# A hybrid layer on one core: the softmax of the next head issued ahead of the transposes and product of this one

## The chip, the core and the metric

The kernel runs on one core of a Trainium2 chip. TensorE (PE) multiplies matrices and writes to PSUM; VectorE (DVE), ScalarE (ACT) and GpSimd (POOL) do the rest, SyncE (SP) issues the loads of weights. Each engine takes its instructions strictly in the order that the program fixed for it. The metric is the time of one execution in microseconds (us), lower is better.

## The reference: what is computed

A decoder layer with two branches over 16 meta tokens and 512 real tokens, all in 32-bit floats. After a norm, one projection `u @ w_in` feeds a Mamba-2 branch (four groups) and an attention branch of 16 heads of 64. The attention is

```
s = q . k / 8 + (cq[t] - ck[s]),  masked to s <= t
p = softmax(s);  o = p @ v;  y_att = o * silu(z_att)
merged = g_ssd * (y_ssd @ w_proj_ssd) + g_att * (y_att @ w_proj_att)
out = x + rmsnorm(merged @ w_out)
```

The softmax goes in blocks of 128 queries: four blocks of real queries, block i with 16 + 128(i+1) keys, of which the first 16 are the meta tokens.

## The kernel before, in words

Every number is split into a high and a low part, and a product is made of three products of parts. The function `gemm` (its matmuls are on line L106) does this for all projections: 24 matmuls of 512 columns for the real tokens (`real_tokens`), 48 of 264 columns for all tokens (`all_tokens`). Its weights come as tiles `raw` (load on SP, L89), are split by ACT into `whi` (L90) and by DVE into `wlo` (L91, 1.2 us each), two buffers each. Its results lie in the PSUM tiles `mm`, of which there are two; a third product starts when the first one has been read.

All else on PE uses the PSUM tiles `ax`, one bank each, of which there are four.

The program runs the four groups of the Mamba-2 branch (`ssd_core`, with the sum of squares on L501 and its spread on L509 at a group's end), then the attention stage, eight pairs of heads (`att_pair`), with products of `s_group` and `gates` in between, then `gates` of the attention, `a_part`, and the output product (L747). The time of each instruction on its engine is fixed by a scheduler before the run, which takes the code's order as priority; parts in `raised()` go first. So while a head's softmax is under way on DVE and ACT, PE is given L106 matmuls of later projections, in an order that is then fixed.

One pair: products for q, k, v and the gate z (`zt`); q and k are evacuated by ACT (L539, L549, L550) and DVE (L540, L551); v is transposed (L558 for the meta tokens, L560). Then, head by head (`att_head`), five score pieces on four `ax` banks (L602 and L603); DVE masks each and takes its maximum (L605); ACT exponentiates (L608); DVE divides by the sum (L615). PE transposes the probabilities: ten blocks of 128x128 (L625), and four times the first 32 columns (L622), which hold the 16 meta columns, into a bank of their own, `t0`. ACT and DVE split the four transposed tiles into high and low parts (L635, L636), POOL zeroes the rest of the meta tile (L633), and nine matmuls (L648) make the product `po`. L582 to L590 gate the result and split it.

Of the kernel before, what the change touches and what calls it, by code (L numbers as in the profile page):

```python
# [37 lines left out]
def hybrid_kernel(ctx, tc, x, meta, norm_pre, w_in, conv_w, conv_b, dt_bias, a_log, d_skip,  # L38
# [490 lines left out]
    def att_pair(pr):  # L529
        heads2 = (2 * pr, 2 * pr + 1)  # L530
        q1, q2, k1, k2 = {}, {}, {}, {}
        ps = real_tokens(wcols(C_Q + pr * P))
# [43 lines left out]
        if pr % 4 == 0:  # L576
            ya[pr // 4] = (st("yhi", [P, 4, T], BUFS["y"], F32R), st("ylo", [P, 4, T], BUFS["y"], F32R))
        yt, lt = row("tmp", (P, T)), row("tmp", (P, T))
        for e in range(2):
            po = att_head(heads2[e], e, q1, q2, k1, k2, vv)  # L580
            m, l = slice(64 * e, 64 * e + 64), slice(64 - 64 * e, 128 - 64 * e)
            S.copy(lt[m], po[l])  # L582
            V.tensor_add(yt[m], po[m], lt[m])
        V.scalar_tensor_tensor(yt, yt, 0.5, zt, op0=ALU.mult, op1=ALU.mult)
        kk = pr % 4
        yh, yl = ya[pr // 4]
        if dbg is not None:
            nc.sync.dma_start(out=dbg["y_att"][pr], in_=yt)
        S.copy(yh[:, kk], yt)
        V.tensor_sub(yl[:, kk], yt, yh[:, kk].bitcast(F32))  # L590

    def att_head(hd, e, q1, q2, k1, k2, vv):
# [49 lines left out]
        for p in (ph, pl):
            seq += [(vv[:, 1, vs], p[1], 0),
                    (vv[:, 2, vs], p[2][:, 0:384], P), (vv[:, 3, vs], p[3], 2 * P),
                    (vv[:, 4, vs], p[2][:, 384:512], 3 * P)]
# [166 lines left out]
```

## Time and profile before

| | us |
|---|---|
| median of 3 runs (lowest, highest) | 861.39 (859.81, 862.04) |
| the profiled execution | 861.74 |
| its span, first to last instruction | 860.0 |
| PE busy in the span | 840.7 |
| DVE busy | 594.4 |
| ACT busy | 433.3 |
| POOL busy | 69.4 |

The profile is of one execution. Matmuls overlap in it: a matmul's row shows the time from its start to its modelled end, and the next one starts before that. What a matmul takes of PE's time is therefore read from the starts of neighbouring rows, not from its own length.

### The profile page before, as it was taken

The page shows a single profiled execution, that of the slowest core. Times are in us where ns is not written, and L with a number is a line of the kernel's source. Part 1 is how long each engine was busy: PE and PEld are TensorE (multiplying, and loading weights), DVE is VectorE, ACT ScalarE, POOL GpSimd, SP SyncE. Part 2 cuts the span into 40 slices and gives each one's busy share as a digit, 9 for nine tenths or more (in the row PEclk, how much of TensorE's full clock was granted, in tenths as well). Part 3 has the DMA queues.
Part 4 walks back from the last instruction along what each step waited for, and adds up shares of the span by engine and source line. Part 5 has one row for each costly group of instructions (what it writes and reads, how often), then busy time and mean ns, then how long its engine had stood idle before and what let it go on. Part 6 is the DMA issues. An engine that isn't in the chain of part 4 may idle for free.

```text
span 860.0 us, 13236 instructions
## 1 busy us (share of the span) xinstructions
PE 840.7 (98%) x5085; PEld 728.2 (85%) x5085; DVE 594.4 (69%) x1216; ACT 433.3 (50%) x834; POOL 69.4 (8%) x136
## 2 busy tenths in 40 slices
PE   6999999999999999999999999999999999999996
PEld 4998888778987799777889898989899988888885
DVE  6799598946985689656766565666667564568735
ACT  6455455446632465334435565656567564543332
POOL 3030110010000100011001000000001000000000
PEclk9999999999999999999999999999999999999999
DMA  7245353335323443212222313232323222224422
GB/s 212 75 130 156 88 105 104 97 81 117 99 84 88 108 113 94 78 50 77 74 74 75 100 51 99 52 98 52 97 55 96 75 74 75 73 74 147 148 74 98
DMA packets 114499, 79.94 MB, mean 93 GB/s; under 512 B 5684, under 2 KB 108260, under 8 KB 114436
## 3 DMA queue, kind: packets, MB, share of 16 engines
q1 hardware_dynamic: 110692, 70.08, 28.4%
q0 software_dynamic: 3744, 9.01, 5.0%
q8 instruction: 40, 0.66, 0.3%
q14 instruction: 23, 0.19, 0.1%
HBM read 76.65 MB, written 2.44 MB: 92 GB/s over the span
## 4 chain that ended last, share of the span: by engine, by line
PE 89%; DVE 4%; DMA 3%; issue 2%; ACT 0%; POOL 0%; SPq 0%; DVEq 0%; POOLq 0%
PE mm L106 70%; PE ax L648 3%; PE mm L747 3%; PE ax L625 2%; DMA big<-acs_d 2%; PE ax L747 1%; PE ax L482 1%; PE ax L467 1%; PE ax L603 1%; PE ax L602 1%; PE ax L457 1%; PE ax L441 1%; PE ax L622 1%; DMA big<-in_x_dram 1%; DVE big L452 1%
## 5 line engine op out<-in xcount | busy, mean ns | idle before, releaser
L106 PE MATMUL mm<-ulo,whi 128*128 128x264 f32 (+1 forms) x1024 | 286.5, 328 | 0.0
L106 PE MATMUL mm<-uhi,whi 128*128 128x264 f32 (+1 forms) x1024 | 283.8, 327 | 0.5 <-DVE xbc L551 0.5
L90 ACT CAST whi<-raw 128x1024 fp32r<-128x1024 f32 x118 | 124.2, 1053 | 151.7 <-PE mm L106 96.5
L106 PE MATMUL mm<-uhi,wlo 128*128 128x264 f32 (+1 forms) x1024 | 189.0, 326 | 0.0
L106 PEld LDWEIGHTS mm<-uhi,whi 128*128 128x128 f32 x1024 | 173.0, 189 | 18.0 <-issue 2.9
L106 PEld LDWEIGHTS mm<-ulo,whi 128*128 128x128 f32 x1024 | 173.1, 189 | 16.5 <-issue 2.7
L91 DVE TENSOR_TENSOR wlo<-raw,whi 128x1024 fp32r<-128x1024 f32 x117 | 142.7, 1220 | 61.0 <-ACT whi L90 32.7
L106 PEld LDWEIGHTS mm<-uhi,wlo 128*128 128x128 f32 x1024 | 153.4, 188 | 15.5 <-issue 0.7
L106 PE MATMUL mm<-yhi,whi 128*128 128x512 f32 x192 | 78.6, 410 | 0.7 <-ACT ms L666 0.7
L106 PE MATMUL mm<-ylo,whi 128*128 128x512 f32 x192 | 76.6, 399 | 0.0
L608 ACT ACTIVATE tmp<-tmp,nmx 128x264 f32<-128x264 f32 (+3 forms) x80 | 41.3, 517 | 32.1 <-DVE nmx L605 27.1
L385 DVE SCALAR_TENSOR_TENSOR xbc<-xp,hcol,xbc 128x528 f32<-128x528 f32 x72 | 54.0, 762 | 0.5 <-ACT tmp L388 0.3
L106 PE MATMUL mm<-yhi,wlo 128*128 128x512 f32 x192 | 53.8, 400 | 0.0
L636 DVE TENSOR_TENSOR big<-ax,big 32x512 fp32r<-32x512 f32 (+1 forms) x64 | 37.3, 616 | 23.2 <-ACT big L635 22.6
L452 DVE TENSOR_SCALAR big<-big,dtok 128x128 f32<-128x128 f32 x128 | 28.4, 286 | 26.7 <-DMA big<-acs_d 26.7
L605 DVE CUSTOM_DVE_ANT_0 tmp<-ax,maskf 128x264 f32<-128x264 f32 (+3 forms) x80 | 32.5, 431 | 20.8 <-PE ax L603 20.4
L461 ACT ACTIVATE tmp<-ax,eac 128x64 f32<-128x64 f32 x128 | 28.2, 330 | 35.2 <-PE ax L457 35.2
L106 PEld LDWEIGHTS mm<-yhi,whi 128*128 128x128 f32 x192 | 36.1, 188 | 10.7 <-issue 2.3
L106 PEld LDWEIGHTS mm<-ylo,whi 128*128 128x128 f32 x192 | 36.1, 188 | 9.4 <-issue 2.6
L106 PEld LDWEIGHTS mm<-yhi,wlo 128*128 128x128 f32 x192 | 35.8, 188 | 9.4 <-issue 2.2
L635 ACT CAST big<-ax 32x512 fp32r<-32x512 f32 (+1 forms) x64 | 28.9, 521 | 26.7 <-PE ax L622 26.6
L668 DVE TENSOR_TENSOR ms<-ms,mm 128x512 f32<-128x512 f32 x24 | 16.5, 686 | 25.4 <-PE mm L106 25.4
(255 smaller groups left out, 1134.0 us busy)
## 6 DMA issues: line engine op xcount, KB each, us to landing
raw<-in_w_in_dram SPq DMA_DIRECT2D x88, 512.0 KB, 3.6
big<-acs_d POOLq DMA_DIRECT2D x16, 512.0 KB, 6.0
raw<-in_w_proj_ssd_dram SPq DMA_DIRECT2D x16, 512.0 KB, 3.3
raw<-in_w_proj_att_dram SPq DMA_DIRECT2D x8, 512.0 KB, 3.4
raw<-in_w_out_dram SPq DMA_DIRECT2D x8, 512.0 KB, 3.4
big<-in_x_dram SPq DMA_DIRECT2D x4, 512.0 KB, 7.1
yhi<-in_x_dram SPq DMA_DIRECT2D x2, 1024.0 KB, 7.3
out_dram<-big SPq DMA_DIRECT2D x3, 512.0 KB, 2.6
```

Of the source, the lines that this page charges most:

```text
L90: S.copy(hi, raw)
L91: (GP if nparts[0] <= 1 else V).tensor_sub(lo, raw, hi.bitcast(F32))
L106: PE.matmul(o, lw, u[:, a:b], start=i == 0, stop=i == len(seq) - 1)
L385: V.scalar_tensor_tensor(o, xp[:, k:k + L], cw[:, 24 * k + ct:24 * k + ct + 1], o, op0=ALU.mult, op1=ALU.add)
L452: V.tensor_scalar(ab[:, i], ab[:, i], ac_t[:, c, g * HG + i:g * HG + i + 1], 0.0, op0=ALU.subtract, op1=ALU.min)
L461: S.activation(y[:, i * 64:(i + 1) * 64], py[:, i * 64:(i + 1) * 64], AF.Copy, scale=eac[:, c, g * HG + i:g * HG + i + 1])
L605: V.tensor_tensor_reduce(pr[i][:, a:b], o, m, -1.0, 3e38, ALU.add, ALU.min, nmx[:, n:n + 1])
L608: S.activation(pr[i][:, a:b], pr[i][:, a:b], AF.Exp, bias=nmx[:, i:i + 1], scale=-1.0, accum_out=rsum[:, n:n + 1])
L635: S.copy(h, src)
L636: V.tensor_sub(l, src, h.bitcast(F32))
L648: PE.matmul(po[:, o:T], w, p, start=i == 0, stop=i == len(seq) - 1)
L747: PE.matmul(pss[s][t], a, b, start=kq == 0 and i == 0, stop=kq == 3 and i == len(seq) - 1)
```

## The change

`att_pair` is taken apart into `att_qk`, `att_v`, `att_z`, `att_soft` (scores and softmax of one head) and `att_head` (transposes, product and evacuation of one head). The main loop writes `att_soft` of a head ahead of `att_head` of the one before it. The first v projection comes ahead of the first q and k; `s_group(3)` comes after the second pair instead of the first, and the `gates` of the SSD branch one pair later.

The five score pieces lie on three `ax` banks instead of four; the last block is cut into 240 and 288 columns instead of 264 and 264.

The meta columns are divided by the sum and split before they are transposed: for each of the four blocks ACT writes 16 high columns and DVE 16 low ones into one tile `mcol` of 128 columns, which one transpose brings into the spare part of bank `t3`. Four copies of 32 partitions (two on ACT, two on DVE) put the four blocks into the zeroed tile `meta`. So that this fits, the meta tokens of v are repeated eight times (`trep`, a copy on POOL) and transposed as 128 columns, which replaces a zeroing on POOL and a copy on ACT. The unused constant `gap` goes.

```diff
--- before.py
+++ after.py
...
+    def att_v(pr):
         ps = all_tokens(wcols(C_V + pr * P))
         t = row("xp", (P, L))
         with raised():
             S.copy(two(t), ps)
         pv, pv0 = ax_ps(), ax_ps()
-        PE.transpose(pv0[0:NM, 0:P], t[:, 0:NM], ident)
+        trep = row("mcol", (P, P))
+        GP.tensor_copy(heads(trep), t[:, 0:NM].unsqueeze(1).broadcast_to([P, HG, NM]))
         for c in range(4):
             PE.transpose(pv[:, c * P:(c + 1) * P], t[:, CH[c + 1][0]:CH[c + 1][1]], ident)
+        PE.transpose(pv0[:, 0:P], trep, ident)
         vv = st("vt", [P, 5, 2 * P], BUFS["vt"], F32R)
-        GP.memset(vv[:, 0].bitcast(F32), 0.0)
-        vm = vv[0:NM, 0]
-        pm, pr_ = pv0[0:NM, 0:P].rearrange("p (e d) -> p e d", e=2), \
+        pm, pr_ = pv0[:, 0:P].rearrange("p (e d) -> p e d", e=2), \
             pv.rearrange("p (c e d) -> p c e d", c=4, e=2)
-        for dst, src in ((vm, pm), (vv[:, 1:5], pr_)):
+        for dst, src in ((vv[:, 1:5], pr_), (vv[:, 0], pm)):
             hi, lo = quarters(dst, 0, 3), quarters(dst, 1, 2)
             S.copy(hi, src)
             V.tensor_sub(lo, src, hi.bitcast(F32))
-        S.copy(vv[32:32 + NM, 0], vm.bitcast(F32))
+        vvs[pr] = vv
+
...
-        pa, pb, pc, pd = ax_ps(), ax_ps(), ax_ps(), ax_ps()
-        pieces = [(pa[:, 0:144], 0, 0, 144), (pa[:, 144:416], 1, 0, 272), (pb[:, 0:400], 2, 0, 400),
-                  (pc[:, 0:HL], 3, 0, HL), (pd[:, 0:HL], 3, HL, L)]
...
+    def att_soft(hd):
+        q1, q2, k1, k2 = qk.pop(hd)
+        pa, pb, pc = ax_ps(), ax_ps(), ax_ps()
+        pieces = [(pa[:, 0:144], 0, 0, 144), (pc[:, 0:272], 1, 0, 272), (pb[:, 0:400], 2, 0, 400),
+                  (pc[:, 272:512], 3, 0, 240), (pa[:, 144:432], 3, 240, L)]
...
-        for n, (o, i, a, b) in enumerate(pieces):
+        for n in (0, 4, 2, 1, 3):
+            o, i, a, b = pieces[n]
             ts_ = slice(i * P, (i + 1) * P)
-            PE.matmul(o, q1[hd][:, ts_], k1[hd][:, a:b], start=True, stop=False)
-            PE.matmul(o, q2[hd][:, ts_], k2[hd][:, a:b], start=False, stop=True)
+            PE.matmul(o, q1[:, ts_], k1[:, a:b], start=True, stop=False)
+            PE.matmul(o, q2[:, ts_], k2[:, a:b], start=False, stop=True)
...
+        mcol = row("mcol", (P, 4, 2, NM), F32R)
         for i in range(4):
             o = pr[i]
+            S.activation(mcol[:, i, 0], o[:, 0:NM], AF.Copy, scale=rinv[:, i:i + 1])
+            V.scalar_tensor_tensor(mcol[:, i, 1], o[:, 0:NM], rinv[:, i:i + 1], mcol[:, i, 0].bitcast(F32),
+                                   op0=ALU.mult, op1=ALU.subtract)
+        for i in range(4):
+            o = pr[i][:, NM:]
             V.tensor_scalar(o, o, rinv[:, i:i + 1], None, op0=ALU.mult)
-        t0, t1, t2, t3 = ax_ps(), ax_ps(), ax_ps(), ax_ps()
+        probs[hd] = pr, mcol
+
+    yls = {}
+
+    def att_head(hd):
+        p, e = hd // 2, hd % 2
+        pr, mcol = probs.pop(hd)
+        t1, t2, t3 = ax_ps(), ax_ps(), ax_ps()
...
-        for i in range(4):
-            PE.transpose(t0[0:32, i * P:(i + 1) * P], pr[i][:, 0:32], ident)
-            for b in range(1, i + 2):
+        for b in (1, 2, 4, 3):
+            for i in range(b - 1, 4):
                 s0 = NM + (b - 1) * P
                 PE.transpose(dest[b, i], pr[i][:, s0:s0 + P], ident)
-        ph, pl = [], []
-        for src in (t0[0:32], t1, t2, t3[:, 0:256]):
-            n, w = src.shape
+        t0 = t3[:, 256:384]
+        PE.transpose(t0, mcol.bitcast(F32).rearrange("p a b c -> p (a b c)"), ident)
+        meta = st("big4", [P, 2, T], BUFS["big4"], F32R)[:, 0]
+        GP.memset(meta.bitcast(F32), 0.0)
+        ph, pl = [None], [None]
+        for src in (t1, t2, t3[:, 0:256]):
+            w = src.shape[1]
             hl = st("big4", [P, 2, T], BUFS["big4"], F32R)
-            h, l = hl[0:n, 0, 0:w], hl[0:n, 1, 0:w]
-            if n == 32:
-                h, l = hl[0:32, 0], hl[32:64, 0]
-                GP.memset(hl[64:128, 0].bitcast(F32), 0.0)
-                meta = hl[:, 0]
+            h, l = hl[:, 0, 0:w], hl[:, 1, 0:w]
             S.copy(h, src)
             V.tensor_sub(l, src, h.bitcast(F32))
             ph.append(h)
             pl.append(l)
+        for i in range(4):
+            r = slice(32 * i, 32 * i + 32)
+            (S.copy if i % 2 else V.tensor_copy)(meta[r, i * P:(i + 1) * P], t0[r])
         po = ax_ps()
...
         seq.append((vv[:, 0, vs], meta, 0))
-        for i, (w, p, o) in enumerate(seq):
-            PE.matmul(po[:, o:T], w, p, start=i == 0, stop=i == len(seq) - 1)
-        return po
+        for i, (w, q, o) in enumerate(seq):
+            PE.matmul(po[:, o:T], w, q, start=i == 0, stop=i == len(seq) - 1)
+        if e == 0:
+            yls[p] = row("tmp", (P, T)), row("tmp", (P, T))
+        yt, lt = yls[p]
...
-    att_pair(0)
-    s_group(3)
-    for pr in range(1, 8):
-        att_pair(pr)
-        if pr < 5:
-            gates(C_GS, 0, g_ssd, range(2 * pr - 2, 2 * pr))
+    att_v(0)
+    for pr in range(8):
+        att_qk(pr)
+        att_soft(2 * pr)
+        if pr:
+            att_head(2 * pr - 1)
+            att_v(pr)
+        att_soft(2 * pr + 1)
+        att_head(2 * pr)
+        att_z(pr)
+        if pr == 1:
+            s_group(3)
+        if 1 < pr < 6:
+            gates(C_GS, 0, g_ssd, range(2 * pr - 4, 2 * pr - 2))
+    att_head(15)
     gates(C_GA, 8, g_att, range(8))
```

Places at which the order of instructions changes. PE at the end of the last group of the Mamba-2 branch, before: L482 closes the group's last chunk, `mm_4182` is the k projection of the first pair, `mm_4249` its v projection, L501 the sum of squares.

```order
L482 MATMUL ax_3924<-big_561_3901,tmp_3899 64x128 x8
L106 MATMUL mm_4182<-uhi_156,whi_4177 128x264 x2
L106 MATMUL mm_4182<-ulo_157,whi_4177 128x264 x2
...
L106 MATMUL mm_4182<-uhi_156,wlo_4178 128x264 x16
L501 MATMUL ax_3956<-onec,tmp_3941 128x1 x4
L106 MATMUL mm_4249<-uhi_156,whi_4244 128x264 x2
```

The same place after (lines are numbered anew: L481 was L482, L500 was L501): `mm_4138` is the v projection, `mm_4209` that of q, `mm_4252` that of k.

```order
L481 MATMUL ax_3923<-big_561_3900,tmp_3898 64x128 x8
L106 MATMUL mm_4138<-uhi_155,wlo_4134 128x264 x16
L106 MATMUL mm_4209<-uhi_155,whi_4204 128x512
...
L106 MATMUL mm_4209<-uhi_155,wlo_4205 128x512 x8
L106 MATMUL mm_4252<-uhi_155,whi_4247 128x264 x2
...
L500 MATMUL ax_3955<-onec,tmp_3940 128x1 x4
L106 MATMUL mm_4252<-ulo_156,whi_4247 128x264 x2
```

Between the two rows stood 48 matmuls of 264 columns; now stand 17 of 264, 24 of 512 and 18 of 264.

DVE at the same place, before: from the last of the four L492 that gate the group's result to what L501 waits for, the third L498.

```order
L492 TENSOR_TENSOR xbc_3502<-xbc_3502,z_3670 128x512
L540 SCALAR_TENSOR_TENSOR z_4165<-mm_4139,xbc_4164 64x512
L498 TENSOR_TENSOR tmp_3941<-tmp_3941,tmp_3945 128x512
L498 TENSOR_TENSOR tmp_3941<-tmp_3941,tmp_3949 128x512
L91 TENSOR_TENSOR wlo_4316<-raw_4314,whi_4315 128x1024
L498 TENSOR_TENSOR tmp_3941<-tmp_3941,tmp_3953 128x512
L540 SCALAR_TENSOR_TENSOR z_4171<-mm_4139,xbc_4170 64x512
```

After (L491 was L492, L497 was L498, L539 was L540):

```order
L491 TENSOR_TENSOR xbc_3501<-xbc_3501,z_3669 128x512
L91 TENSOR_TENSOR wlo_4248<-raw_4246,whi_4247 128x1024
L497 TENSOR_TENSOR tmp_3940<-tmp_3940,tmp_3944 128x512
L497 TENSOR_TENSOR tmp_3940<-tmp_3940,tmp_3948 128x512
L497 TENSOR_TENSOR tmp_3940<-tmp_3940,tmp_3952 128x512
L91 TENSOR_TENSOR wlo_4448<-raw_4446,whi_4447 128x1024
L539 SCALAR_TENSOR_TENSOR z_4235<-mm_4209,xbc_4234 64x512
L502 TENSOR_SCALAR gms_3961<-ax_3955 128x4
```

The split of weights (L91) that stood ahead of the last of the three sums stands behind it, and both evacuations of q stand behind the sums.

PE in the third pair, before: from the start of one head's transposes to the first matmul of its product.

```order
L106 MATMUL mm_5553<-ulo_157,whi_5548 128x512
L106 MATMUL mm_5553<-uhi_156,whi_5548 128x512
L622 MATMUL ax_5353<-ident,tmp_5322 32x128
L625 MATMUL ax_5354<-ident,tmp_5322 128x128
L622 MATMUL ax_5353<-ident,tmp_5322 32x128
...
L625 MATMUL ax_5356<-ident,tmp_5324 128x128
L625 MATMUL ax_5355<-ident,tmp_5324 128x128
...
L648 MATMUL ax_5384<-big_813_5375,vt_5273 128x512
L648 MATMUL ax_5384<-big_814_5378,vt_5273 128x384
```

After, in the fourth pair: `ax_5282` is the third score bank of the next head, `ax_5326` and `ax_5327` are the second and third transposed tiles of this one, `ax_5354` its product.

```order
L631 MATMUL ax_5326<-ident,tmp_5125 128x128
L631 MATMUL ax_5326<-ident,tmp_5126 128x128
L631 MATMUL ax_5326<-ident,tmp_5127 128x128 x2
L595 MATMUL ax_5282<-xbc_5114,xbc_5047 128x240
L596 MATMUL ax_5282<-xbc_5115,z_5048 128x240
L631 MATMUL ax_5327<-ident,tmp_5126 128x128
L631 MATMUL ax_5327<-ident,tmp_5127 128x128
L633 MATMUL ax_5327<-ident,mcol_5152 128x128
L106 MATMUL mm_5476<-uhi_155,wlo_5472 128x512 x3
L657 MATMUL ax_5354<-big_804_5341,vt_5275 128x512
```

The 14 transposes in a row have become 11 in groups, with scores of the next head and projections between them.

## Rows read from the trace of the kernel before

**Rows 1.** The page: span, and each engine's busy us, share and instructions.
```profile
span 860.0 us, 13236 instructions
...
PE 840.7 (98%) x5085; PEld 728.2 (85%) x5085; DVE 594.4 (69%) x1216; ACT 433.3 (50%) x834; POOL 69.4 (8%) x136
```

**Rows 2.** Window of the attention stage: us, busy us (instructions) by engine, PEclk, DMA share, GB/s.
```profile
404.00:700.00 296.00, 293.46 (x1825) 264.59 (x1824) 191.19 (x423) 172.09 (x348) 23.27 (x49) 0.99 0.28 75
```

**Rows 3.** Timeline of PE, one head's 14 transposes between projections: start, length, line, operands.
```profile
534.31 0.39 PE L106 MATMUL mm<-uhi,whi 128*128 128x512 f32 x1
...
534.76 0.40 PE L106 MATMUL mm<-uhi,whi 128*128 128x512 f32 x1
535.00 0.27 PE L622 MATMUL ax<-ident,tmp 128*32 128x128 f32 x1
...
536.76 0.39 PE L106 MATMUL mm<-uhi,whi 128*128 128x512 f32 x1
```

**Rows 4.** Groups by line and form, 437 to 700 us: busy, mean ns | idle, releaser.
```profile
L622 PE MATMUL ax<-ident,tmp 128*32 128x128 f32 x48 | 12.4, 272 | 0.0
...
L636 DVE TENSOR_TENSOR big<-ax,big 32x512 fp32r<-32x512 f32 x12 | 8.2, 680 | 13.6 <-ACT big L635 13.4
...
L635 ACT CAST big<-ax 32x512 fp32r<-32x512 f32 x12 | 6.9, 576 | 17.2 <-PE ax L622 17.1
...
L570 ACT CAST vt<-vt 16x256 fp32r<-16x256 f32 x6 | 2.4, 406 | 1.8 <-DVE vt L569 1.7
...
L569 DVE TENSOR_TENSOR vt<-ax,vt 16x128 fp32r<-16x128 f32 x6 | 1.7, 279 | 14.5 <-ACT vt L568 14.5
...
L568 ACT CAST vt<-ax 16x128 fp32r<-16x128 f32 x6 | 1.5, 255 | 3.9 <-PE ax L558 3.8
```

**Rows 5.** Timeline of PE, end of the last SSD group, with what ended the wait.
```profile
404.56 0.40 PE L106 MATMUL mm<-ulo,whi 128*128 128x264 f32 x2
404.80 2.08 PE L106 MATMUL mm<-uhi,wlo 128*128 128x264 f32 x16
408.95 1.02 PE L501 MATMUL ax<-onec,tmp 128*128 128x1 f32 x8 [2.07 <-DVE tmp L498]
```

**Rows 6.** Window behind that wait, columns as in rows 2.
```profile
410.00:414.00 4.00, 4.00 (x21) 4.00 (x21) 3.37 (x15) 1.09 (x2) 0.00 (x0) 0.57 0.29 101
```

**Rows 7.** Timeline of DVE at the end of the last SSD group.
```profile
401.01 1.12 DVE L487 SCALAR_TENSOR_TENSOR xbc<-xbc,dcol,ax 128x128 f32<-128x128 f32 x4
402.05 2.49 DVE L492 TENSOR_TENSOR xbc<-xbc,z 128x512 f32<-128x512 f32 x4
404.45 0.68 DVE L540 SCALAR_TENSOR_TENSOR z<-mm,xbc 64x512 fp32r<-64x512 f32 x1
...
406.98 1.23 DVE L91 TENSOR_TENSOR wlo<-raw,whi 128x1024 fp32r<-128x1024 f32 x1 [0.45 <-PE mm L106]
408.12 0.69 DVE L498 TENSOR_TENSOR tmp<-tmp,tmp 128x512 f32<-128x512 f32 x1
```

**Rows 8.** Timeline of PE, its last wait in the attention stage.
```profile
699.36 0.47 PE L106 MATMUL mm<-uhi,whi 128*128 128x512 f32 x1 [0.47 <-DVE xbc L551]
```

**Rows 9.** Timeline of PE, a transpose alone, and four behind products.
```profile
397.68 0.49 PE L106 MATMUL mm<-uhi,wlo 128*128 128x512 f32 x1
...
398.03 1.40 PE L106 MATMUL mm<-uhi,wlo 128*128 128x512 f32 x5
...
519.34 0.80 PE L648 MATMUL ax<-big,vt 128*128 128x384 f32 x4
519.97 0.60 PE L560 MATMUL ax<-ident,xp 128*128 128x128 f32 x4
```

**Rows 10.** Timelines of ACT and of DVE, small instructions in a row.
```profile
385.06 1.76 ACT L461 ACTIVATE tmp<-ax,eac 128x64 f32<-128x64 f32 x8 [4.11 <-PE ax L457]
...
410.90 0.16 DVE L193 SCALAR_TENSOR_TENSOR grst<-grs 128x4 f32<-128x4 f32 x1
411.10 0.16 DVE L194 TENSOR_TENSOR grst<-grst,gms 128x4 f32<-128x4 f32 x1
```

More of the change, by code (lines that the diff above doesn't have):

```diff
@@ L30 @@
 EPS = 1e-6
-BUFS = {"tmp": 10, "xbc": 13, "z": 4, "xp": 2, "h": 2, "big4": 4, "raw": 3, "whi": 2, "wlo": 2, "y": 2, "vt": 2}
+BUFS = {"tmp": 10, "xbc": 13, "z": 4, "xp": 2, "h": 2, "big4": 4, "raw": 3, "whi": 2, "wlo": 2, "y": 2, "vt": 2, "mcol": 3}
 C_Z, C_XS, C_B, C_C = 0, 2048, 4096, 4608
@@ L129, in hybrid_kernel @@
     onec = cst.tile([P, 1], F32, name="onec")
-    cst.tile([P, 96], F32, name="gap")
     GP.memset(onec, 1.0)
@@ L527, in quarters, with att_qk @@
         return v[..., i:j + 1:j - i, :]
-    def att_pair(pr):
-        heads2 = (2 * pr, 2 * pr + 1)
-        q1, q2, k1, k2 = {}, {}, {}, {}
+    qk, vvs, zts = {}, {}, {}
+    def att_qk(pr):
         ps = real_tokens(wcols(C_Q + pr * P))
-        for e, hd in enumerate(heads2):
+        for e, hd in enumerate((2 * pr, 2 * pr + 1)):
             r = slice(64 * e, 64 * e + 64)
@@ L541, in att_pair @@
                                        op1=ALU.subtract)
-            q1[hd], q2[hd] = a, b
+            qk[hd] = [a, b]
         ps = all_tokens(wcols(C_K + pr * P))
-        for e, hd in enumerate(heads2):
+        for e, hd in enumerate((2 * pr, 2 * pr + 1)):
             r = slice(64 * e, 64 * e + 64)
@@ L551, in att_pair @@
                 V.tensor_sub(two(a[64:128]), ps[r], two(a[0:64].bitcast(F32)))
-            k1[hd], k2[hd] = a, b
+            qk[hd] += [a, b]
+    def att_v(pr):
         ps = all_tokens(wcols(C_V + pr * P))
@@ L569, in att_pair, with att_z @@
             V.tensor_sub(lo, src, hi.bitcast(F32))
-        S.copy(vv[32:32 + NM, 0], vm.bitcast(F32))
+        vvs[pr] = vv
+    def att_z(pr):
         ps = real_tokens(wcols(C_ZA + pr * P))
@@ L575, in att_pair @@
             V.scalar_tensor_tensor(zt, zt, 1.0, ps, op0=ALU.add, op1=ALU.mult)
[L576 to L592, printed above, removed]
-        pa, pb, pc, pd = ax_ps(), ax_ps(), ax_ps(), ax_ps()
-        pieces = [(pa[:, 0:144], 0, 0, 144), (pa[:, 144:416], 1, 0, 272), (pb[:, 0:400], 2, 0, 400),
-                  (pc[:, 0:HL], 3, 0, HL), (pd[:, 0:HL], 3, HL, L)]
+        zts[pr] = zt
+    probs = {}
+    def att_soft(hd):
[3 more added lines that the diff above has]
+                  (pc[:, 272:512], 3, 0, 240), (pa[:, 144:432], 3, 240, L)]
         nmx = st("nmx", [P, 5], 2)
@@ L612, in att_head @@
         V.reciprocal(rinv, rsum[:, 0:4])
+        mcol = row("mcol", (P, 4, 2, NM), F32R)
         for i in range(4):
             o = pr[i]
-            V.tensor_scalar(o, o, rinv[:, i:i + 1], None, op0=ALU.mult)
-        t0, t1, t2, t3 = ax_ps(), ax_ps(), ax_ps(), ax_ps()
+            S.activation(mcol[:, i, 0], o[:, 0:NM], AF.Copy, scale=rinv[:, i:i + 1])
[3 more added lines that the diff above has]
+            o = pr[i][:, NM:]
+            V.tensor_scalar(o, o, rinv[:, i:i + 1], None, op0=ALU.mult)
+        probs[hd] = pr, mcol
[3 more added lines that the diff above has]
+        pr, mcol = probs.pop(hd)
+        vv = vvs[p]
+        t1, t2, t3 = ax_ps(), ax_ps(), ax_ps()
         dest = {(1, 0): t1[:, 0:128], (1, 1): t1[:, 128:256], (1, 2): t1[:, 256:384],
@@ L641, in att_head @@
         seq = []
[L642 to L645, printed above, removed]
+        for q in (ph, pl):
+            seq += [(vv[:, 1, vs], q[1], 0),
+                    (vv[:, 2, vs], q[2][:, 0:384], P), (vv[:, 3, vs], q[3], 2 * P),
+                    (vv[:, 4, vs], q[2][:, 384:512], 3 * P)]
         seq.append((vv[:, 0, vs], meta, 0))
-        for i, (w, p, o) in enumerate(seq):
-            PE.matmul(po[:, o:T], w, p, start=i == 0, stop=i == len(seq) - 1)
-        return po
+        for i, (w, q, o) in enumerate(seq):
[3 more added lines that the diff above has]
+        yt, lt = yls[p]
+        m, l = slice(64 * e, 64 * e + 64), slice(64 - 64 * e, 128 - 64 * e)
+        S.copy(lt[m], po[l])
+        V.tensor_add(yt[m], po[m], lt[m])
+        if e == 0:
+            return
+        V.scalar_tensor_tensor(yt, yt, 0.5, zts[p], op0=ALU.mult, op1=ALU.mult)
+        if p % 4 == 0:
+            ya[p // 4] = (st("yhi", [P, 4, T], BUFS["y"], F32R), st("ylo", [P, 4, T], BUFS["y"], F32R))
+        kk = p % 4
+        yh, yl = ya[p // 4]
+        if dbg is not None:
+            nc.sync.dma_start(out=dbg["y_att"][p], in_=yt)
+        S.copy(yh[:, kk], yt)
+        V.tensor_sub(yl[:, kk], yt, yh[:, kk].bitcast(F32))
     msd = [None] * KD
```

## Prediction

> **What bounds the kernel now.** The page says that PE is busy for 840.7 of 860.0 us [rows 1], but a matmul's row overlaps the next, so a busy PE can still wait or run slowly. The window of the attention stage comes next: from 404 to 700 us PE is idle for 296.00 - 293.46 = 2.54 us [rows 2]. The timeline of PE puts nearly all of it at two places, 2.07 us ahead of L501 [rows 5] and 0.47 us at 699 us [rows 8]. DVE is busy for 191 and ACT for 172 of the same 296 us [rows 2]. So in this stage PE works through a fixed list of matmuls, and what DVE and ACT do is covered by projections. A softmax that is issued earlier has nothing to hide there but those 2.54 us. The change can help only by taking work from PE, or at these two places.
>
> What one matmul takes of PE is read from starts. Two projections of 512 columns start 0.45 us apart over two steps [rows 3], 0.225 each; two of 264 take 0.24 [rows 5], 0.12 each. Between 535.00 and 536.76 lie 14 transposes and one projection of 512 [rows 3]: (1.76 - 0.225) / 14 = 0.110 us for a transpose, whether it has 32 stationary columns or 128.
>
> **The change part by part.**
>
> *Transposes.* Each of 16 heads has four L622; one transpose of `mcol` takes their place. 48 fewer at 0.110 us are **-5.3 us**. The row of L622 gives 272 ns as the length of one [rows 4], but the next one starts after 0.110, so the length is overlap. [...] If it were the price, 48 of them would give 13.1 us; this is a rival below. The v transposes stay five in a pair, the scores keep their 1344 columns per head (240 + 288 for 264 + 264), and the nine product matmuls stay: nothing.
>
> *The end of the Mamba-2 branch.* Before, PE has 48 matmuls of 264 columns between L482 and L501, 48 x 0.12 = 5.8 us of work from about 401 us. L501 needs the third L498 on DVE. From 401.01 DVE does four L487 and four L492, a L540, two L498, and then a L91 that starts at 406.98 because it waited for the end of that same projection; the last L498 follows at 408.12 and ends at 408.81 [rows 7], and PE goes on at 408.95 [rows 5]. The wait is 2.07 us. [...]
>
> After, PE has 17 x 0.12 + 24 x 0.225 + 18 x 0.12 = 9.6 us between the same two points. DVE needs 1.12 + 2.49 for the first eight, 1.23 for one L91, whose whole cover is the v projection that ended long before, and 3 x 0.69 = 2.1 for the sums: 6.9 us. ACT's squares start behind the first L492 (now L491) and run beside it. That leaves 2.7 us of slack, and PE should not stop: **-2.07**, and with the wait the slow clock goes, **-1.72**. What is late next? The projection of z (`mm_4452`) takes the PSUM tile of q, which the second L539 on DVE must have read. PE reaches it 9.6 + 1.0 (L501 [rows 5]) + 30 x 0.12 = 14.2 us after L481. Q's product ends after 2.0 + 5.4 = 7.4, and two evacuations of a head by ACT and DVE follow; before, the first L540 ended at 405.13, behind all of L492 [rows 7], some 4 us after the k projection began (404.80 + 1.92 - 5.76 = 401.0). With 5 us for both it is free at 12.5, and at 14 if it must wait longer in DVE's queue: covered, by little.
>
> *The wait at 699 us.* It is for an evacuation of k (L551) that stood late in DVE's order. With the softmax of another head in between the order is a different one: I take **-0.47**, bounds 0 and -0.47.
>
> *Interleaving.* The 14 transposes in a row become groups. In the program's order I count 31 stretches of transposes on PE from the k projection of the first pair on before, and 55 after. One between projections costs 398.03 - 397.68 = 0.35 against 0.225 + 0.110, 0.015 more; four behind products start 0.63 us after 1280 columns that take 0.56 at 0.225 per 512, 0.07 more [rows 9]. 24 more at 0.015 to 0.07 are 0.4 to 1.7 us; most stand next to projections, so **+0.6**.
>
> *Small instructions.* ACT gets 64 of 128x16 and 32 copies of 32x128, DVE the same. The nearest rows: eight of 128x64 on ACT in 1.76 us, 0.22 each, and 128x4 on DVE every 0.20 us [rows 10]; copies of 16x128 from PSUM 0.26 and 0.28 [rows 4]. That is 64 x 0.22 + 32 x 0.26 = 22.4 us on ACT, 64 x 0.20 + 32 x 0.28 = 21.8 on DVE. What goes: 16 x 0.58 (L635) and 8 x 0.41 (L570) on ACT, 16 x 0.68 (L636) on DVE [rows 4]. Net about +10 on ACT and +11 on DVE, or 182 and 202 of some 290 us: still under PE. Where that cover is gone, it costs what the fifth part prices. [...] POOL gets a copy per pair and loses a zeroing; both lie far ahead of their use.
>
> *New waits.* Three score banks and three transposed tiles share four banks, so a product must take the bank of the next head's last score piece, once DVE has read it. In the order that is shown, PE does two transposes, the meta one and three projections in between: 3 x 0.110 + 3 x 0.225 = 1.0 us. DVE's reading is one mask-and-maximum, under 0.5 us, if DVE is free. The same sum for all 16 heads gives 1.0 and 1.1 us at two of them and 2.3 us or more at the others. Below: no wait. Above: a L91 of 1.23 us in front at both, 2.5 us. The nearest row is the whole stage of before, with 0.47 us of waits in 290; I take **+0.5**.
>
> Sum: -5.3 - 2.07 - 1.72 - 0.47 + 0.6 + 0.5 = -8.4. The profiled execution took 861.74, which is 0.35 above the median of 861.39; against the median the forecast is **853.0 us**.
>
> **The rivals.**
>
> *A: as above.* With the bounds, -9.5 + 0.4 and -9.1 + 1.7 + 2.5, that is 852.3 to 856.5; half a microsecond that no row shows below. Chance 0.70.
>
> *B: the wait at the end of the Mamba-2 branch stays,* at L501 or at the z projection, where the cover is thin. Then 3.8 us are not gained: 856.8. For it: 14.2 us against 12.5 to 14; against it: 2.7 us of slack at L501. Chance 0.08.
>
> *C: PE waits at many heads,* 0.3 to 0.7 us each, for a bank or a transposed tile that DVE or ACT has not read, since both have 10 us more to do and work on two heads at once: 857.5 to 863. For it: the small instructions; against it: the share of DVE, 70%, and the two tight heads out of 16. Chance 0.12, half of it under 858.8.
>
> *D: slower than before.* The same bank hand-off, at every head, behind a split of weights: 1.23 us x 16 = 19.7, less 9.5, plus a slow clock behind some of them: 873. It decides from 0.75 us a head (12 us in all). For it: DVE takes its instructions in a fixed order with 1.23 us pieces among them; against it: 14 heads have a cover above 2 us. Chance 0.06.
>
> *E: a transpose costs PE what its row says.* 48 x 0.272 = 13.1 instead of 5.3: 845. The starts speak against it. Chance 0.04.
>
> That the change does nothing would need the transposes to be hidden; PE has no idle time in which they could be.
>
> **How the numbers follow.** 853.0 is A's. The range 851.5 to 858 holds A, B and half of C, some 0.83. About 0.3%, or 2.6 us, is what a measurement of this kernel can tell from no change. Faster by more (under 858.8): A, B, E and half of C, 0.88. Within it: the rest of C, 0.06. Slower: D, 0.06.
>
> **What would show it.** Right: no idle time of PE at the end of the Mamba-2 branch and a granted clock of 1.00 there; transposes still 0.11 us apart, 16 of `mcol`; DVE near 605 and ACT near 443 us busy; PE idle for less than 2 us in the stage. Wrong: idle time of PE ahead of the first product of a head with DVE's mask (L598) as releaser (C, D); a slow clock between 395 and 425 us (B); a stage that is shorter by 13 us (E). The forecast fails above all if two heads in flight make DVE's order late in a way that its share of busy time doesn't show.

## The result, and the profile after

The changed kernel takes **853.14 us** (median of 4 runs, 853.14 to 853.55), the kernel before 861.71 beside it: a ratio of 0.9905, 95% interval 0.9888 to 0.9922. The forecast was 853.0. The change is faster by about 1%, and the number is right. The experiments below show that one of the reasons behind it is not.

The page of the changed kernel, span and busy time by engine, against [rows 1]:

```profile
span 851.4 us, 13318 instructions
...
PE 834.7 (98%) x5037; PEld 722.9 (85%) x5037; DVE 601.8 (71%) x1296; ACT 442.5 (52%) x906; POOL 72.1 (8%) x136
```

The span is 8.6 us shorter, with 48 matmuls fewer on PE. DVE has 7.4 us more to do and ACT 9.2 us more. The window of the attention stage, against [rows 2] (us, then busy us of PE, PEld, DVE, ACT and POOL, then the granted clock):

```profile
404.00:700.00 296.00, 296.00 (x1825) 265.90 (x1824) 204.87 (x519) 185.17 (x425) 25.50 (x51) 1.00 0.29 78
```

PE is never idle there, where before it was idle for 2.54 us, and the mean granted clock is 1.00, against 0.99. The timeline of PE at the end of the Mamba-2 branch, against [rows 5] and [rows 6]:

```profile
408.94 0.40 PE L106 MATMUL mm<-uhi,whi 128*128 128x264 f32 x2
409.18 0.95 PE L500 MATMUL ax<-onec,tmp 128*128 128x1 f32 x8
...
411.76 2.08 PE L106 MATMUL mm<-uhi,wlo 128*128 128x264 f32 x16
413.69 0.40 PE L106 MATMUL mm<-uhi,whi 128*128 128x512 f32 x1
```

and of DVE, against [rows 7]:

```profile
402.95 1.22 DVE L91 TENSOR_TENSOR wlo<-raw,whi 128x1024 fp32r<-128x1024 f32 x1
404.09 2.28 DVE L497 TENSOR_TENSOR tmp<-tmp,tmp 128x512 f32<-128x512 f32 x3
...
410.56 0.69 DVE L539 SCALAR_TENSOR_TENSOR z<-mm,xbc 64x512 fp32r<-64x512 f32 x1
```

The three sums (L497) end at 406.37, and PE reaches their reader L500 at 409.18, so there are 2.8 us to spare (forecast 2.7). The second evacuation of q ends at 411.25, and the z projection that needs its tile begins at 413.69, with 2.4 us to spare. Neither row of PE has a wait. The transposes of the last head, against [rows 3]:

```profile
738.66 1.26 PE L631 MATMUL ax<-ident,tmp 128*128 128x128 f32 x10
739.76 0.27 PE L633 MATMUL ax<-ident,mcol 128*128 128x128 f32 x1
```

Ten transposes start within 1.10 us, 0.110 each, as before.

### The profile page after: what moved, and what is told of

Same layout as the page of the kernel before. It is cut to its first block, busy times and chain, and to the rows that moved or that the text cites. A ratio compares the mean times of both kernels' runs of the same rounds, so it can differ in the third digit from the quotient of the medians.

```text
span 851.4 us, 13318 instructions
## 1 busy us (share of the span) xinstructions
PE 834.7 (98%) x5037; PEld 722.9 (85%) x5037; DVE 601.8 (71%) x1296; ACT 442.5 (52%) x906; POOL 72.1 (8%) x136
## 4 chain that ended last, share of the span: by engine, by line
PE 90%; DMA 3%; DVE 3%; issue 2%; ACT 0%; POOL 0%; SPq 0%; DVEq 0%; POOLq 0%
PE mm L106 71%; PE ax L657 3%; PE mm L781 3%; PE ax L631 2%; DMA big<-acs_d 2%; PE ax L781 1%; PE ax L481 1%; PE ax L596 1%; PE ax L466 1%; PE ax L595 1%; PE ax L456 1%; PE ax L440 1%; DMA big<-in_x_dram 1%; DVE big L451 1%; PE ax L477 1%
## 5 line engine op out<-in xcount | busy, mean ns | idle before, releaser
L106 PE MATMUL mm<-ulo,whi 128*128 128x264 f32 (+1 forms) x1024 | 286.5, 328 | 0.0
L106 PE MATMUL mm<-uhi,whi 128*128 128x264 f32 (+1 forms) x1024 | 284.5, 327 | 0.0
L91 DVE TENSOR_TENSOR wlo<-raw,whi 128x1024 fp32r<-128x1024 f32 x117 | 142.8, 1220 | 68.4 <-ACT whi L90 31.5
L106 PE MATMUL mm<-uhi,wlo 128*128 128x264 f32 (+1 forms) x1024 | 189.4, 326 | 0.0
L106 PEld LDWEIGHTS mm<-uhi,whi 128*128 128x128 f32 x1024 | 172.3, 188 | 16.9 <-issue 2.7
L106 PEld LDWEIGHTS mm<-ulo,whi 128*128 128x128 f32 x1024 | 172.4, 188 | 16.3 <-issue 2.9
L106 PEld LDWEIGHTS mm<-uhi,wlo 128*128 128x128 f32 x1024 | 152.6, 188 | 14.5 <-issue 0.7
L106 PE MATMUL mm<-yhi,whi 128*128 128x512 f32 x192 | 78.6, 409 | 0.7 <-ACT ms L691 0.7
L106 PE MATMUL mm<-ylo,whi 128*128 128x512 f32 x192 | 76.6, 399 | 0.0
L601 ACT ACTIVATE tmp<-tmp,nmx 128x400 f32<-128x400 f32 (+4 forms) x80 | 41.2, 517 | 28.1 <-DVE nmx L598 26.0
L106 PE MATMUL mm<-yhi,wlo 128*128 128x512 f32 x192 | 54.1, 401 | 0.0
L598 DVE CUSTOM_DVE_ANT_0 tmp<-ax,maskf 128x288 f32<-128x288 f32 (+4 forms) x80 | 32.7, 434 | 23.3 <-PE ax L596 23.0
L106 PEld LDWEIGHTS mm<-yhi,whi 128*128 128x128 f32 x192 | 36.1, 188 | 10.7 <-issue 2.3
L106 PEld LDWEIGHTS mm<-ylo,whi 128*128 128x128 f32 x192 | 36.1, 188 | 9.5 <-issue 2.6
L106 PEld LDWEIGHTS mm<-yhi,wlo 128*128 128x128 f32 x192 | 35.8, 188 | 9.2 <-issue 2.2
L657 PE MATMUL ax<-big,vt 128*128 128x512 f32 (+2 forms) x144 | 35.4, 329 | 0.0
L453 ACT ACTIVATE big<-big 128x1024 f32<-128x1024 f32 x16 | 17.0, 1061 | 33.9 <-DVE big L451 33.9
```

The lines of the kernel that those rows point to most:

```text
L91: (GP if nparts[0] <= 1 else V).tensor_sub(lo, raw, hi.bitcast(F32))
L106: PE.matmul(o, lw, u[:, a:b], start=i == 0, stop=i == len(seq) - 1)
L453: S.activation(ab, ab, AF.Exp)
L598: V.tensor_tensor_reduce(pr[i][:, a:b], o, m, -1.0, 3e38, ALU.add, ALU.min, nmx[:, n:n + 1])
L601: S.activation(pr[i][:, a:b], pr[i][:, a:b], AF.Exp, bias=nmx[:, i:i + 1], scale=-1.0, accum_out=rsum[:, n:n + 1])
L657: PE.matmul(po[:, o:T], w, q, start=i == 0, stop=i == len(seq) - 1)
```

## The experiments

Two readings recur in all of them: when the product of the last head ends (the start of its last matmul), and how many L106 matmuls PE still has behind that (the column "left": rows of L106 that start later, in the profiled run).

| kernel | median us | ratio to before, 95% | last product ends at | left |
|---|---|---|---|---|
| before | 861.71 | 1 | 784 | 108 |
| after | 853.14 | 0.9905 [0.9888, 0.9922] | 748 | 231 |
| `t48` | 857.99 | 0.9963 [0.9951, 0.9976] | 747 | 255 |
| `small2` | 853.27 | 0.9905 [0.989, 0.992] | 749 | 231 |
| `qk_first` | 857.59 | 0.994 [0.9924, 0.9957] | 751 | 231 |
| `ahead` | 861.44 | 1.000 [0.999, 1.0011] | 755 | 247 |
| `v_first` | 864.41 | 1.0017 [1.0005, 1.0029] | 785 | 108 |
| `v_first_s` | 856.60 | 0.9943 [0.993, 0.9956] | 771 | 144 |
| `meta` | 870.11 | 1.0089 [1.0074, 1.0105] | 793 | 84 |
| `in_turn` | 880.11 | 1.02 [1.018, 1.022] | 803 | 84 |
| `before_small` | 879.56 | 1.0209 [1.0192, 1.0225] | 804 | 84 |
| `meta_v_s` | 863.92 | 1.0014 [0.9999, 1.0029] | 785 | 84 |
| after, again | 854.07 | 0.9895 [0.9873, 0.9918] | 749 | 231 |

The kernel before was measured anew beside each later group of runs, with medians of 862.29, 861.35, 861.53 and 862.64; each ratio is to the one measured beside it.

### One part undone or alone: the first theory

My theory was the prediction's: the terms are independent, and the early softmax hides nothing. The rival: the early softmax is what pays.

**`t48`** puts 48 transposes back into the changed kernel, and nothing else:

```diff
+        for i in range(3):
+            PE.transpose(t3[0:32, 384:512], pr[i + 1][:, 0:32], ident)
```

> The changed kernel with three transposes of 32 stationary columns more in each head, 48 in all, into a spare part of a transposed tile that nobody reads; what they replaced is otherwise not there, so no other engine has more to do. My theory (0.110 us each of PE's time): 853.1 + 5.3 = 858.4 us (857.8 to 859.2). Rival (0.272 us each, as their rows say): 866.2. A third possibility (they find room in idle time): 853.5 or less.

It takes 0.9963 - 0.9905 = 0.0058 of 861.35, or 5.0 us more than the changed kernel: 0.104 us a transpose (0.101 by the medians). With the two intervals that is some 3 to 7 us, far from the 13 us of rival E of the prediction, which falls. The row of the added ones still says 272 ns:

```profile
L635 PE MATMUL ax<-ident,tmp 128*32 128x128 f32 x48 | 7.9, 272 | 0.0
```

**`small2`** issues the small instructions on ACT and DVE twice in the changed kernel:

```diff
-        for i in range(4):
+        for i in (0, 0, 1, 1, 2, 2, 3, 3):
             o = pr[i]
             S.activation(mcol[:, i, 0], ...
```

> The changed kernel with each of the small instructions that divide and split the meta columns issued twice: 64 more of 128x16 on ACT and 64 more on DVE, the same result. That doubles the suspected cost: ACT near 457 us busy, DVE near 613. My theory (both lie under PE's projections): 853.1 to 853.8 us. Rival (DVE or ACT comes late for PE when two heads are under way): 14 us more work in 16 heads shows as waits ahead of transposes or products, 856 or more.

It takes 853.27 us: they cost nothing, though ACT is busy for 13 us and DVE for 10 us more. The page of this run:

```profile
PE 833.1 (98%) x5037; PEld 721.0 (85%) x5037; DVE 611.6 (72%) x1360; ACT 455.6 (53%) x970; POOL 72.0 (8%) x136
```

**`qk_first`** writes the first q and k ahead of the first v again:

```diff
+    att_qk(0)
     att_v(0)
     for pr in range(8):
-        att_qk(pr)
+        if pr:
+            att_qk(pr)
```

> The changed kernel with q and k of the first pair ahead of its v, as before the change; the rest as changed. My theory: the wait ahead of the sum of squares and the slow clock behind it come back, 853.1 + 3.8 = 856.9 us (856.2 to 857.6). Rival (the early softmax moves DVE's order by itself, so the wait stays away): 853.0 to 853.6.

It takes 857.59 us, as my theory had it at its upper end: 4.5 us more than the changed kernel by the medians, 3.0 by the ratios. PE's timeline of this kernel has the old wait back, to the same length:

```profile
410.26 0.91 PE L500 MATMUL ax<-onec,tmp 128*128 128x1 f32 x7 [2.07 <-DVE tmp L497]
```

In the windows of the same run the clock behind it is not slow:

```profile
404.00:410.30 6.30, 4.23 (x36) 4.05 (x35) 5.72 (x10) 5.66 (x9) 3.07 (x6) 1.00 0.29 81
410.00:416.00 6.00, 5.74 (x48) 5.77 (x49) 4.61 (x17) 1.78 (x3) 0.00 (x0) 1.00 0.32 87
```

This run took 856.47, the shortest of six; the four at 857.59 or more had a mean clock of 0.993 to 0.995 over the whole span, this one 0.997. In the kernel before, with the same wait of 2.07 us [rows 5], the mean clock is 0.95 from 395 to 430 us and 0.99 from 404 to 700 [rows 2]. It is 0.99 also in `ahead` from 404 to 700 us and in `meta` from 404 to 680, where PE is idle for 2.07 us in all, and in `before_small` from 404 to 680, where it is idle for 3.67; here it is 1.00 from 404 to 700, with 2.07 us idle.

**`meta`** is the kernel before with the new meta columns (`mcol`, one transpose, `trep`) and nothing else; **`in_turn`** is the changed kernel with `att_soft` of a head directly ahead of its own `att_head`:

```diff
         att_qk(pr)
+        if pr:
+            att_v(pr)
         att_soft(2 * pr)
-        if pr:
-            att_head(2 * pr - 1)
-            att_v(pr)
-        att_soft(2 * pr + 1)
         att_head(2 * pr)
         att_z(pr)
+        att_soft(2 * pr + 1)
+        att_head(2 * pr + 1)
...
-    att_head(15)
```

> The kernel before with one part of the change: the meta columns go through one transpose, 48 transposes fewer; four score banks, heads in turn, q and k of the first pair ahead of v as before. My theory (a transpose costs PE 0.11 us wherever it stands, and the wait at the end of the Mamba-2 branch is a matter of order): 861.7 - 5.3 = 856.4 us, 855.5 to 857.5 with the small instructions under PE's cover; PE still waits some 2 us ahead of the sum of squares and the granted clock still falls behind it. Rival 1 (the early softmax is what pays): within 0.5 us of 861.7. Rival 2 (a transpose costs the 0.272 us of its row): 848.6.

> The changed kernel with its heads in turn: each softmax is written directly ahead of its own transposes and product; one meta transpose, three score banks and v first stay. My theory (PE has projections to put under a softmax in either order, so the early softmax hides nothing): within 1 us of the changed kernel, 852.0 to 854.0; it may be 0.5 lower, for fewer changes between kinds of matmul, or have one wait of 0.5 at 699 us back. Rival 1 (the early softmax pays): PE waits for the softmax or the transposed tiles at several heads, 856 or more.

Both expectations fail, by 14 and 27 us. `meta` has the same 48 transposes fewer as the changed kernel and is slower than before by 7.8 us. PE's timeline of `meta` at the last head's product (L654) and behind it:

```profile
790.45 0.40 PE L654 MATMUL ax<-big,vt 128*128 128x512 f32 x1
...
791.42 1.08 PE L654 MATMUL ax<-big,vt 128*128 128x256 f32 x6 [0.28 <-ACT big L638]
793.05 0.47 PE L654 MATMUL ax<-big,vt 128*128 128x512 f32 x1 [0.55 <-ACT big L644]
796.30 0.73 PE L106 MATMUL mm<-yhi,whi 128*128 128x512 f32 x2 [2.77 <-ACT yhi L587]
```

and in `in_turn`:

```profile
794.34 0.28 PE L596 MATMUL ax<-xbc,z 68*128 68x240 f32 x1
797.92 2.42 PE L631 MATMUL ax<-ident,tmp 128*128 128x128 f32 x10 [3.30 <-ACT mcol L609]
...
806.44 1.22 PE L106 MATMUL mm<-yhi,whi 128*128 128x512 f32 x2 [2.77 <-ACT yhi L673]
```

In `in_turn` PE goes from the last scores straight to a wait for the softmax, then to a wait for the split result of the last pair (`yhi`): nothing else stands between them in its order. The windows of the late heads of `meta`, `in_turn` and the kernel before:

```profile
680.00:810.00 130.00, 122.73 (x618) 104.37 (x617) 82.52 (x198) 63.98 (x146) 4.14 (x9) 0.96 0.25 78
```

```profile
640.00:820.00 180.00, 165.16 (x856) 141.37 (x855) 108.34 (x268) 88.98 (x208) 7.49 (x16) 0.94 0.23 71
```

```profile
680.00:805.00 125.00, 124.53 (x663) 107.01 (x662) 80.52 (x159) 60.73 (x116) 2.90 (x6) 1.00 0.30 92
```

PE of `meta` is idle for 7.3 us there, and by an estimate from the mean clock loses 0.04 x 130 = 5.2 us to the slow clock. Less 5.0 for the transposes and 0.5 for the wait of before at 699 us, that is 7.0 of the 7.8. PE of `in_turn` is idle for 14.8 us and by the same estimate loses 0.06 x 180 = 10.8: 25.6 of its 27.

Half of this idle time lies ahead of 700 us, 3.7 us in `meta` and 7.3 in `in_turn`, while 455 to 600 L106 matmuls are still to come. In `meta` PE's timeline has it at the scores of the twelfth head, which wait for DVE to read a product's bank, and at the v projection of the last pair, which waits for DVE to read q:

```profile
687.63 0.39 PE L600 MATMUL ax<-xbc,xbc 128*128 128x264 f32 x1 [2.35 <-DVE tmp L581]
...
689.78 0.81 PE L106 MATMUL mm<-uhi,whi 128*128 128x264 f32 x2 [1.31 <-DVE z L539]
```

The kernel before has its 0.47 us at the projection behind that one, z of the last pair [rows 8].

**`v_first`** is the kernel before with the v part of the first pair ahead of q and k:

```diff
+        if pr == 0:
+            vv = att_v(pr)
         ps = real_tokens(wcols(C_Q + pr * P))
```

> The kernel before with the v projection of the first pair ahead of its q and k, and nothing else. The stretch of PE around the sum of squares is then the one of the changed kernel (17 matmuls of 264 columns, 24 of 512, 18 of 264), all heads are as before. My theory: the wait of 2.07 us and the 1.72 us of slow clock go, 861.7 - 3.8 = 857.9 us (857.3 to 858.6), granted clock 1.00 from 395 to 425 us. Rival (the wait went because the first softmax runs ahead, not because of v): the wait stays somewhere, 861.0 or more.

It takes 864.41 us, which is the rival, and is 0.4 to 2.5 us slower than before by the interval. The wait at the sum of squares (L501) is gone, and three others stand at the first head and at `s_group(3)`, here in PE's timeline:

```profile
422.07 0.42 PE L609 MATMUL ax<-xbc,xbc 128*128 128x400 f32 x1 [0.66 <-DVE xbc L513]
...
424.13 0.39 PE L609 MATMUL ax<-xbc,xbc 128*128 128x272 f32 x1 [0.85 <-DVE nmx L612]
...
431.33 0.50 PE L106 MATMUL mm<-yhi,whi 128*128 128x512 f32 x1 [0.78 <-DVE ms L675]
```

They are 2.3 us, for the 2.07 that went; 0.46 us at 700 us stay as well. The mean clock from 404 to 700 us is 1.00 in spite of them.

### Heads in turn as a chain: the second theory

So the parts don't add up. The second theory: heads in turn are a chain, each head's scores following the product of the head before. From the first score to the end of the last product, the kernel before needs (784 - 424) / 16 = 22.5 us a head. PE fills the gaps of the chain with projections, of which there is a fixed number. At 84 left PE has run out of those that it can do. The last `a_part` (the results of the last four pairs times their projection weights) is eight products of 12 matmuls, 96 in all, and in each of the two `mm` tiles six matmuls stand ahead of the first that needs the last pair's result: 96 - 12 = 84. That result comes 3.2 us after the start of the product's last matmul (793.05 to 796.30 in `meta`), and only what is left above 84 covers that. The kernel before had 108 - 84 = 24 of them, 24 x 0.225 = 5.4 us, the changed kernel 147. Whatever makes the chain longer uses the matmuls up, and PE waits. The early softmax has two heads under way and shortens the chain to (748 - 419) / 16 = 20.6 us a head. The rival: it is the later transpose and copies of the meta columns, not the chain, that made `meta` slow.

**`ahead`** is the changed kernel without the meta columns and with q and k of the first pair ahead of v. Beside the early softmax, its three score banks and its cut of the scores it so keeps the later `s_group(3)` and gates, which its expectation does not say. **`before_small`** is the kernel before with the small instructions added, into a tile that nobody reads:

```diff
+        mcol = row("mcol", (P, 4, 2, NM), F32R)
+        for i in range(4):
+            o = pr[i]
+            S.activation(mcol[:, i, 0], o[:, 0:NM], AF.Copy, scale=rinv[:, i:i + 1])
+            V.scalar_tensor_tensor(mcol[:, i, 1], o[:, 0:NM], ...)
         for i in range(4):
             o = pr[i]
             V.tensor_scalar(o, o, rinv[:, i:i + 1], None, op0=ALU.mult)
```

> The kernel before with only the softmax issued ahead: three score banks, each softmax ahead of the transposes and product of the head before; four meta transposes in a head in a bank of their own and q and k ahead of v, as before. The second theory, formed after the first runs: heads in turn are one chain of some 22 us a head that ends at 784 us with little to spare, the early softmax takes two heads off it at a time and makes room, but PE had no idle time, so alone it gives nothing: 861 to 863.5 us, last product near 750. Rival (the early softmax pays by itself): 858.5 or less. A risk: five banks wanted by transposes and product beside three score banks make PE wait, 865 or more.

> The kernel before with the small instructions of the change added ahead of the division, into a tile that nobody reads: 64 more of 128x16 on ACT and 64 on DVE; transposes, banks and order of code as before. In the changed kernel the same doubling cost nothing. Second theory (without the early softmax each head's chain is on the path): a head takes 1 us or more longer, the last product ends at 790 us or later, PE waits at the last heads, 864 to 872 us. Rival (ACT and DVE are covered here too, and what slowed the meta-only kernel were its later transpose and copies): 861.0 to 862.5.

`ahead` gives 1.000: without the meta columns the early softmax, with the later `s_group(3)` and gates beside it, is worth nothing, though its last product ends 29 us sooner and 247 matmuls are left behind it.

`ahead` and `qk_first` differ by the meta columns alone, apart from the order of a head's ten other transposes, as the kernel before and `meta` do. So the same part is measured twice: with heads in turn it costs 0.0089 of the time, 7.7 us, and with the early softmax it gains 1.000 - 0.994 = 0.006, 5.2 us.

`before_small` is 18.0 us slower, by the same instructions that cost nothing in `small2`. A head takes (804 - 424) / 16 = 23.75 us there, 1.25 more; the rows of ACT and of DVE have 0.90 and 0.67 us for the four small instructions of a head on each:

```profile
796.00 0.90 ACT L615 ACTIVATE mcol<-tmp,rinv 128x16 fp32r<-128x16 f32 x4
```

```profile
798.00 0.67 DVE L616 SCALAR_TENSOR_TENSOR mcol<-tmp,rinv,mcol 128x16 fp32r<-128x16 f32 x4
```

The groups of PE behind the last product, in the kernel before (from 784.3 us), where no row waits:

```profile
L106 PE MATMUL mm<-ylo,whi 128*128 128x512 f32 x36 | 14.0, 389 | 0.0
L106 PE MATMUL mm<-yhi,whi 128*128 128x512 f32 x36 | 13.9, 390 | 0.0
L106 PE MATMUL mm<-yhi,wlo 128*128 128x512 f32 x36 | 9.6, 389 | 0.0
```

and in `before_small` (from 803.4 us):

```profile
L106 PE MATMUL mm<-ylo,whi 128*128 128x512 f32 x26 | 10.8, 414 | 0.0
L106 PE MATMUL mm<-yhi,whi 128*128 128x512 f32 x26 | 10.1, 394 | 2.8 <-ACT yhi L588 2.8
L106 PE MATMUL mm<-yhi,wlo 128*128 128x512 f32 x32 | 9.7, 430 | 0.0
```

These are 3 x 36 = 108 against 26 + 26 + 32 = 84, and the 84 begin with the wait. The window of the late heads has 10.95 us idle, and by the estimate from the mean clock loses 0.04 x 180 = 7.2, together about the 18 us:

```profile
640.00:820.00 180.00, 169.05 (x912) 145.69 (x911) 113.36 (x263) 92.78 (x207) 7.71 (x16) 0.96 0.25 74
```

The longest of these waits does not lie at the end, and the count of what is left does not explain it. Here 503 L106 matmuls are still to come:

```profile
682.36 0.81 PE L106 MATMUL mm<-uhi,whi 128*128 128x264 f32 x2 [3.96 <-DVE h L574]
```

What does hold for the slower kernels is that the time follows the end of the chain. Against the kernel before, the last product ends 1.0 us later in `v_first`, 8.9 in `meta`, 19.0 in `in_turn` and 19.5 in `before_small`; the spans are 1.1, 8.4, 19.1 and 18.9 us longer.

**`v_first_s`** adds to `v_first` the later `s_group(3)` and gates of the change:

```diff
-    att_pair(0)
-    s_group(3)
-    for pr in range(1, 8):
+    for pr in range(8):
         att_pair(pr)
-        if pr < 5:
-            gates(C_GS, 0, g_ssd, range(2 * pr - 2, 2 * pr))
+        if pr == 1:
+            s_group(3)
+        if 1 < pr < 6:
+            gates(C_GS, 0, g_ssd, range(2 * pr - 4, 2 * pr - 2))
```

> The kernel with v first, and in addition the last product of the Mamba-2 branch (s_group(3)) after the second pair and the gates one pair later, as in the change; heads in turn, four meta transposes. Theory: v first took the wait at the sum of squares away, and the 2.4 us of waits at the first head and at s_group(3) came in its place because s_group(3) was all that PE had there; with other projections in between they go: 857.9 us (857.3 to 858.6). Rival (the wait is for the branch's last results, whatever stands between): 861 or more. If moving s_group(3) takes cover from the later heads, waits show there and the time is 859 to 864.

It takes 856.60 us, 4.9 us less than before (3.8 to 6.0 by the interval). From 404 us to the end of the last head PE has no wait and a mean clock of 1.00:

```profile
404.00:771.00 367.00, 367.00 (x2199) 326.45 (x2198) 234.73 (x520) 207.69 (x422) 22.38 (x47) 1.00 0.29 77
```

With `s_group(3)` and the gates later, the last product also ends sooner, with 144 - 84 = 60 matmuls to spare. Which of the two moves does it was not separated.

### Without the early softmax altogether

If room at the end is all that is needed, `v_first_s` should bear the meta columns too, and be a little faster than the changed kernel. **`meta_v_s`** is `v_first_s` with the edit of `meta`.

> Everything of the change but the early softmax and its three score banks: one meta transpose, v first, s_group(3) and the gates later; heads in turn, four score banks. With v first and s_group(3) later the last head's product ended at 771 us instead of 784; the meta columns alone made it end 9 us later than before, at 793. Second theory (PE waits only when the last product comes later than some 785 us): 780 us, no waits, 856.6 - 5.2 = 851.4 us (850.8 to 852.5), a little better than the changed kernel. Rival (with the small instructions on its chain a head in turn is too slow wherever the stage begins): waits at the last heads, 860 or more.

It takes 863.92 us, 12.5 us more than I expected: the rival. My 785 us as the point behind which PE waits was wrong (the product ends at 785 and PE waits). The count was not: with 84 matmuls left there is no cover. The 60 matmuls to spare, 60 x 0.225 = 13.5 us, are used up by heads that take (785 - 419) / 16 = 22.9 us instead of 22.0. PE's timeline of the last head:

```profile
780.12 1.62 PE L635 MATMUL ax<-ident,tmp 128*128 128x128 f32 x10 [2.00 <-ACT mcol L621]
...
788.46 1.22 PE L106 MATMUL mm<-yhi,whi 128*128 128x512 f32 x2 [2.77 <-ACT yhi L594]
```

The mean clock from 775 to 800 us is 0.80, by estimate 5 us lost beside 5.1 idle:

```profile
775.00:800.00 25.00, 19.90 (x78) 15.32 (x78) 16.97 (x37) 9.68 (x23) 0.00 (x0) 0.80 0.31 105
```

> The changed kernel again, beside the one above: 853.1 us within 0.6.

It takes 854.07 us, with a ratio of 0.9895, whose interval holds the first ratio. No version here beats the changed kernel.

## Why the prediction was right, and where its reason was not

*Transposes, -5.3.* The term is right in size and mechanism when the early softmax is there (`t48`: 5.0; `qk_first` against `ahead`: 5.2). It is not independent: `meta` has the same term and loses 7.8.

*The end of the Mamba-2 branch, -2.07 and -1.72, and the 0.47 at 699 us.* `v_first_s` has these three and gains 4.9, against 4.3 predicted. But the prediction gave 3.8 of it to v ahead of q and k, and nothing to the later `s_group(3)` and gates: without them, `v_first` only trades 2.07 us of waits for 2.3. The 0.47 went in `v_first_s` without the softmax of another head in between, to which the prediction put it. No run shows the 1.72 us as a time of its own; it is an estimate, 4 x 0.43 from the mean of 0.57 over 4 us [rows 6]. The runs show a mean clock of 1.00 from 404 us to the end of the last head without the wait (`v_first_s`), and in `qk_first` the wait with 1.00 over the 6 us from 410 us. What the two terms have as 3.8 is 4.5 us there by the medians and 3.0 by the ratios. The slow clock came with the wait in the kernel before and not in this run: it is not a fixed companion.

*Interleaving, +0.6, and new waits, +0.5.* There are no new waits. The span fell by 8.6; 2.54 of waits, 1.7 of clock by the estimate from 0.57 and 5.0 of transposes are 9.2, so about 0.6 is left for all else, interleaving with it. With the interval of `t48` that can't be told from nothing. The two tight bank hand-offs held.

*Small instructions.* DVE is busy for 601.8 and ACT for 442.5 us, against 605 and 443. "Still under PE" held in the changed kernel, but the reason given for it failed. I read it from the share of busy time, 202 of some 290 us. That share says nothing of a chain: in `before_small` DVE is busy for 69% of the span, and the same instructions cost 18 us. They are covered in the changed kernel because two heads are under way.

*"A softmax that is issued earlier has nothing to hide there but those 2.54 us."* For the kernel before this is borne out by `ahead`, to 0.1% and with the later `s_group(3)` and gates in it, and it misled all the same. PE had hardly any idle time, but only 24 matmuls stood between that and waiting at the end. The early softmax gives no time by itself; it gives the room in which the meta columns cost nothing: without it, the changed kernel takes 880.11 us (`in_turn`). Of rivals A to E the outcome is A; that the parts need each other was in none.

*The number.* That 853.0 lies within 0.2 us of the median is partly luck. Single terms were off by 0.3 to 0.5 us and partly made up for each other, and the interval of the gain is 6.7 to 9.7 us. The larger luck is that the change brought the early softmax along, for which the prediction had no use. (The terms add up to -8.46; the prediction has -8.4.)

*What stays open.* The order is fixed before the run. How much of a longer chain lies in that order and how much arises in the run was not separated. Nor is it shown why, with heads in turn, PE waits at 650 to 700 us with hundreds of projections still to come, or what makes `in_turn`, with three score banks, another cut of the scores and the z projection between its heads, 16 us slower than `meta_v_s`. No run has the early softmax without the later `s_group(3)` and gates, so whether it makes enough room without them is not known.

## What to carry to other kernels

An engine without idle time can still be about to wait: count what it has left behind the last piece of the longest chain, and how much of that doesn't need the chain's result. The count shows how near the end is to waiting; it does not show waits in the middle. An edit that shortens a busy engine's list but lengthens a chain can lose; pair it with one that shortens the chain, even if that one by itself measures as nothing. Price parts together, or build each part alone before trusting a sum.
